# Output projection by one level of Strassen, in a hybrid attention layer on one core

## The chip, the core and the metric

The kernel runs on one core of one Trainium2 chip. Its engines have queues of their own, in order: TensorE (PE in the profile, PEld its weight loads), VectorE (DVE), ScalarE (ACT), GpSimd (POOL) and SyncE (SP), which here issues nearly all DMA transfers. Matmuls write to PSUM; GpSimd has only SBUF operands in this kernel. The metric is the device time of one execution in microseconds.

## The reference

One layer of a decoder trunk, in float32: 1024 tokens, model width 2048, batch 1. `x` is normalised, projected to 6656 columns, and goes through two groups of 16 heads (stick-breaking attention and sliding-window attention with sinks and a relative bias). What matters here is the end:

```python
o_sb = rmsnorm(o_sb, gn_sb[l]) * jax.nn.silu(z_sb)
o_sw = rmsnorm(o_sw, gn_sw[l]) * jax.nn.silu(z_sw)
y = jnp.einsum('bse,ed->bsd', jnp.concatenate([o_sb, o_sw], axis=-1), w_out[l])
h = h + rmsnorm(y, norm_post[l])
```

Each `rmsnorm` divides a token's row by its root mean square over the width (1024 for a group, 2048 for y) and multiplies it with a gain. So a group's norm gives one factor per token and group.

## The kernel before

The kernel is written with a tile framework: the program names tiles from pools (a tag with a number of buffers), and the framework places them, sets the semaphores, and orders each engine's queue at build time, by the order in the program and by when its own model has the operands ready. Matmuls issued through `mm` (line 105) keep the program's order; those of the output projection (line 681) have no such mark.

**Precision.** Every float32 matmul that matters is done as three matmuls in the type float32r. An operand is cast on ScalarE (`hi`), the residual is formed on VectorE (`lo` = raw - hi), and hi x hi, hi x lo and lo x hi are accumulated in PSUM.

**Before the output projection.** Lines 258 to 657 do the input projection block by block (`proj`, 52 blocks of 128 columns) with the attention units woven between. x stands in SBUF as 32 tiles `xh0` ... `xl15` of pool `xp`, whose space the output projection uses again. The last blocks of the input projection are gates `z_sb`. `evac_z` (329) multiplies a head pair's output by gain and SiLU gate, writes it to DRAM as `ogd[tile]` (16 tiles of 128 mixed columns, by 1024 tokens), and sums squares into `accs` (GpSimd). The group factor is not applied there: `group_rms` (350) turns `accs` into `ssw` and `ssb`, [128 tokens, 8 blocks], with 8 one-column matmuls for each group.

**The output projection** (lines 635 to 790) runs over two halves of the tokens (`th`), four blocks of 512 model columns (`dc`), the two groups (`gi`: mixed tiles 8 to 15 are the sliding-window group, 0 to 7 the stick-breaking one), 8 tiles `e` of a group and 4 token tiles `tb` of 128:
- `split_wo` (638) loads a block [128 mixed, 512 model] of `w_out`, casts it (645) and forms the residual (647). It is called two or three blocks ahead of the matmuls. Three raw buffers (`wraw`), four pairs of hi and lo.
- `load_og` (666) loads a tile of gated attention outputs for half the tokens and splits it the same way. All 16 tiles of a half stay in SBUF.
- `mm_out` (678) issues three matmuls with 128 tokens as the stationary operand and 512 model columns moving. Four PSUM banks collect the 8 tiles of a group; eight banks in all.
- `evac_sw` (704) copies the first group's sum out of PSUM times the token's factor `ssw` (ScalarE, 707); `evac_sb` (710) adds the second group's sum times `ssb` (VectorE, 719), squares the row with a running sum (ScalarE, 720), and multiplies by the post-norm gain `gp` (GpSimd, 721).
- `finish` (723) forms the row factor of y, loads x (`xr`, two staging buffers `u`), multiplies, adds (737) and stores (738). It runs for the first half's tokens after `th` = 0, for the others tile by tile at the end.
- For the last column block of the second half, `hold_w` (693) keeps all 16 weight blocks in SBUF, so that the last loop can go token tile by token tile; the very last sum goes in two parts of 256 columns.

Weight blocks are loaded and split again for the second half of the tokens: 128 loads and splits in all.

## Time and profile before

| | |
|---|---|
| median of 3 runs | 1888.94 us (1888.36 to 1891.02) |
| the profiled execution: its own time | 1889.21 us |
| its span in the trace | 1887.5 us |
| mean granted TensorE clock | 0.991 |
| DMA over the span | 236.94 MB, 126 GB/s |
| instructions | 26831 |

The span is that of the instructions; the execution's own time has a little around it. Busy times of engines add up what an engine worked on, side by side with the others; they say where work is, not what sets the time. What sets it is read from TensorE's idle times and what ended them, and from the chain of waits that ends last. Matmuls overlap: each is shown with some 0.39 us, but they follow each other more closely, so their cost is the distance between starts.

### The profile page before, as it was taken

How to read it: one execution, taken by the hardware profiler on the slowest of the kernel's cores; microseconds unless marked ns; L12 is line 12 of the kernel's file. 1: busy time of each engine (PE TensorE's matmuls, PEld its weight loads, DVE VectorE, ACT ScalarE, POOL GpSimd, SP SyncE). 2: the span in 40 equal slices, each digit the busy share in tenths (PEclk: the TensorE clock that was granted, in tenths of full speed). 3: DMA queues.
4: the chain of work that ended last, by engine and by line, in shares of the span. 5: the costliest groups of instructions: out<-in, count | busy, mean ns of one | idle time of the engine just before them, and what ended most of it. 6: DMA issues, size and time to landing. Idle time of an engine off the chain costs nothing.

```text
span 1887.5 us, 26831 instructions
## 1 busy us (share of the span) xinstructions
PE 1832.6 (97%) x9262; PEld 1533.1 (81%) x9262; DVE 1156.8 (61%) x1905; ACT 776.0 (41%) x1654; POOL 402.2 (21%) x440
## 2 busy tenths in 40 slices
PE   8799999999999999999999999999999999998997
PEld 6678888888888878888888888888888778886776
DVE  8548842688277685785667756577686743344433
ACT  6335531455244343443434444344343443332331
POOL 7411010101023141141221311113144311111111
PEclk9899999999999999999999999999999999999999
DMA  6545542455333243343333423334234743347435
GB/s 212 169 127 166 142 140 84 121 147 153 94 110 120 73 134 101 94 123 89 116 105 100 119 80 116 106 96 126 80 119 133 259 148 103 97 131 211 127 92 156
DMA packets 167255, 236.94 MB, mean 126 GB/s; under 512 B 21936, under 2 KB 81488, under 8 KB 166992
## 3 DMA queue, kind: packets, MB, share of 16 engines
q1 hardware_dynamic: 165056, 232.09, 42.6%
q10 hardware_dynamic: 2064, 3.15, 0.5%
q8 instruction: 73, 1.20, 0.3%
q14 instruction: 62, 0.51, 0.1%
HBM read 171.19 MB, written 63.96 MB: 125 GB/s over the span
## 4 chain that ended last, share of the span: by engine, by line
PE 77%; DMA 10%; DVE 6%; issue 2%; POOL 2%; ACT 2%; SPq 1%; DVEq 0%; ACTq 0%; POOLq 0%
PE p_ksb L110 9%; PE y L681 9%; PE p_qsb L110 9%; PE p_vsb L110 9%; PE p_qsw L110 8%; PE p_zsw L110 8%; PE p_zsb L110 6%; PE o_sb L110 4%; PE z_sb L110 4%; DMA woraw<-in_w_out 3%; DMA xr<-in_x 3%; PE wt_sb L114 3%; PE z_sw L110 2%; PE o_sw L110 2%; DVE m_sb L450 1%
## 5 line engine op out<-in xcount | busy, mean ns | idle before, releaser
L681 PE MATMUL y<-wohi,og 128*128 128x512 f32 x896 | 282.0, 394 | 7.5 <-ACT wohi L645 7.5
L681 PEld LDWEIGHTS y<-wohi,og 128*128 128x128 f32 x896 | 170.3, 190 | 46.4 <-ACT wohi L645 11.4
L450 DVE TENSOR_TENSOR_SCAN m_sb<-m_sb,zero 128x256 f32<-128x256 f32 x192 | 165.3, 902 | 62.3 <-ACT m_sb L439 61.2
L681 PE MATMUL y<-wolo,og 128*128 128x512 f32 x448 | 178.8, 399 | 8.9 <-DVE wolo L647 8.9
L439 ACT ACTIVATE m_sb<-z_sb 128x512 f32<-128x512 f32 x160 | 96.2, 601 | 148.6 <-PE z_sb L110 142.1
L647 DVE TENSOR_TENSOR wolo<-woraw,wohi 128x512 fp32r<-128x512 f32 x112 | 85.3, 770 | 112.6 <-ACT wohi L645 112.6
L445 POOL TENSOR_SCALAR_AFFINE_SELECT b_sb<-b_sb 128x512 f32<-128x512 f32 x64 | 49.9, 779 | 449.9 <-ACT b_sb L441 449.9
L450 DVE TENSOR_TENSOR_SCAN m_sb<-m_sb,mask 128x256 f32<-128x256 f32 x128 | 115.5, 939 | 43.8 <-ACT m_sb L439 43.3
L645 ACT CAST wohi<-woraw 128x512 fp32r<-128x512 f32 x112 | 68.5, 620 | 140.5 <-PE y L681 102.4
L454 DVE TENSOR_TENSOR b_sb<-b_sb,m_sb 128x512 f32<-128x512 f32 x160 | 111.0, 694 | 17.9 <-POOL b_sb L445 5.7
L721 POOL TENSOR_TENSOR y<-y,gp 128x512 f32<-128x512 f32 (+1 forms) x33 | 46.4, 1432 | 319.7 <-ACT y L720 319.7
L681 PEld LDWEIGHTS y<-wolo,og 128*128 128x128 f32 x448 | 85.2, 190 | 33.8 <-DVE wolo L647 16.6
L110 PE MATMUL p_zsw<-xh,whi_zsw 128*128 128x512 f32 x256 | 104.8, 409 | 0.0
L110 PE MATMUL p_ksb<-xh,whi_ksb 128*128 128x512 f32 x256 | 104.4, 408 | 0.0
L110 PE MATMUL p_qsb<-xh,whi_qsb 128*128 128x512 f32 x256 | 104.4, 408 | 0.0
L110 PE MATMUL p_zsb<-xh,whi_zsb 128*128 128x512 f32 x256 | 102.9, 402 | 0.0
L110 PE MATMUL p_vsb<-xh,whi_vsb 128*128 128x512 f32 x256 | 102.7, 401 | 0.0
L110 PE MATMUL p_zsw<-xh,wlo_zsw 128*128 128x512 f32 x256 | 101.1, 395 | 0.0
L110 PE MATMUL p_zsw<-xl,whi_zsw 128*128 128x512 f32 x256 | 101.0, 395 | 0.0
L110 PE MATMUL p_qsb<-xh,wlo_qsb 128*128 128x512 f32 x256 | 100.8, 394 | 0.0
L110 PE MATMUL p_ksb<-xh,wlo_ksb 128*128 128x512 f32 x256 | 100.7, 393 | 0.0
L110 PE MATMUL p_qsb<-xl,whi_qsb 128*128 128x512 f32 x256 | 100.6, 393 | 0.0
(237 smaller groups left out, 4786.7 us busy)
## 6 DMA issues: line engine op xcount, KB each, us to landing
woraw<-in_w_out SPq DMA_DIRECT2D x128, 256.0 KB, 3.2
kh<-kd SPq DMA_DIRECT2D x160, 64.0 KB, 2.5
kl<-kd SPq DMA_DIRECT2D x160, 64.0 KB, 2.5
q_sw<-qd SPq DMA_DIRECT2D x64, 128.0 KB, 3.2
od<-ot_sw SPq DMA_DIRECT2D x128, 64.0 KB, 2.2
or_zsw<-od SPq DMA_DIRECT2D x16, 512.0 KB, 4.1
wraw_qsb<-in_w_blk SPq DMA_DIRECT2D x32, 256.0 KB, 3.3
wraw_ksb<-in_w_blk SPq DMA_DIRECT2D x32, 256.0 KB, 3.1
```

The costliest lines, as they stand in the source:

```text
L110: tc.keep_in_program_order(nc.tensor.matmul(ps, a, b, start=start, stop=stop))
L114: tc.keep_in_program_order(nc.tensor.transpose(ps, a, ident))
L439: nc.scalar.activation(m[:, :, 1:257], z, AF.Sigmoid, scale=-SCALE)
L445: nc.gpsimd.affine_select(out=beta, in_=beta, compare_op=ALU.is_gt, fill=0.0, base=0, pattern=[[-P, 2], [1, 256]], channel_multiplier=-1)
L450: nc.vector.tensor_tensor_scan(m[:, tb, 1:257], m[:, tb, 1:257], mask[:, P - P * tb:P - P * tb + 256] if prev is None else zero.to_broadca ...
L454: nc.vector.tensor_mul(beta, beta, m[:, :, 0:256])
L645: nc.scalar.copy(wh, raw)
L647: nc.vector.tensor_sub(wl, raw, wh.bitcast(F32))
L681: nc.tensor.matmul(ps, ogt[:, a, cols], w, start=(first and i == 0), stop=(last and i == 2))
L721: nc.gpsimd.tensor_mul(yc, yc, gp[:, dc * HALF:(dc + 1) * HALF][:, part])
```

## The change

The output projection becomes one level of Strassen's scheme. The token halves (512 tokens), the halves of the mixed width (the two groups, 1024 each) and the halves of the model width (1024) make quarters of both operands; seven products of quarter sums replace the eight quarter products.
- The factors of the group norms can no longer be applied per group while evacuating, since sums run across groups. So `group_rms` now makes rows: a matmul of an all-ones [128, 128] tile (the first 128 columns of `mask`, all ones there) with `accs` gives each partition the factor of every token, [128, 1024] for each group; the attention outputs are multiplied with it when they are loaded.
- `PRODUCTS` lists, for each product, the quarters of x and their sign, those of the weights and theirs, and the quarters of y that it goes to, with sign and whether it is the last contribution.
- `split_wo` loads one or two parts of `w_out`; two are added or subtracted on GpSimd ahead of cast and residual. Two-part blocks have four pair buffers (two for the first eight blocks).
- `load_quarter` loads the four quarters of x once (products 1 and 2) and multiplies them with the factor rows, on VectorE and GpSimd in turn. `make_x` forms the sum (VectorE), cast and residual of an operand tile for the next product, in the second half of a product; 9 tiles.
- `evac` copies a first contribution to y out of PSUM (ScalarE) and adds or subtracts later ones (VectorE); a last contribution is followed by square and gain.
- `finish` runs for the second token half after product 6, for the first one tile by tile in the last half product. The last half product has 8 weight tiles of its own in place of `hold_w`.

The diff, cut to its core:

```diff
-    ssw = const.tile([P, 8], F32, name="ssw")
-    ssb = const.tile([P, 8], F32, name="ssb")
+    row_sw = const.tile([P, S], F32, name="row_sw")
+    ones = mask[:, :P]
...
-    def group_rms(grp, dst):
-        ps = pz(f"rms_{grp}")
-        for i in range(8):
-            mm(ps[:, i:i + 1], accs[grp][:, i * P:(i + 1) * P], one, start=True, stop=True)
-        nc.scalar.activation(dst, ps[:, 0:8], AF.Sqrt, bias=eps, scale=1.0 / 1024)
-        nc.vector.reciprocal(dst, dst)
+    def group_rms(grp, row):
+        for h in range(2):
+            cols = slice(h * HALF, (h + 1) * HALF)
+            ps = pz(f"rms_{grp}_{h}")
+            mm(ps, ones, accs[grp][:, cols], start=True, stop=True)
+            nc.scalar.activation(row[:, cols], ps, AF.Sqrt, bias=eps, scale=1.0 / 1024)
+            nc.vector.reciprocal(row[:, cols], row[:, cols])
...
-                defer(12.0, lambda: group_rms("sw", ssw))
+                defer(12.0, lambda: group_rms("sw", row_sw))
...
-    wo_list = [(th, dc, e) for th in range(2) for dc in range(4 - th) for e in list(range(8, 16)) + list(range(8))]
-    wo_ready = {}
...
+    Q_W = {"11": (8, 0), "12": (8, 1), "21": (0, 0), "22": (0, 1)}
+    Q_X = {"11": (8, 0), "12": (0, 0), "21": (8, 1), "22": (0, 1)}
+    PRODUCTS = [
+        (("11",), ("12", -1, "22"), (("12", 1, 0), ("22", 1, 0))),
+        (("21", -1, "11"), ("11", 1, "12"), (("22", 1, 0),)),
+        (("11", 1, "12"), ("22",), (("12", 1, 1), ("11", -1, 0))),
+        (("21", 1, "22"), ("11",), (("21", 1, 0), ("22", -1, 0))),
+        (("22",), ("21", -1, "11"), (("21", 1, 1), ("11", 1, 0))),
+        (("11", 1, "22"), ("11", 1, "22"), (("22", 1, 1), ("11", 1, 0))),
+        (("12", -1, "22"), ("21", 1, "22"), (("11", 1, 1),)),
+    ]
+    LAST = len(PRODUCTS) - 1
+    w_list = [(i, dc, e) for i in range(LAST + 1) for dc in range(2) for e in range(8)]
+    w_ready = []
+    out_pools = {}
+
+    def w_part(dst, quarter, dc, e):
+        e0, half = Q_W[quarter]
+        col = half * 2 * HALF + dc * HALF
+        nc.sync.dma_start(dst, w_out[(e0 + e) * P:(e0 + e + 1) * P, col:col + HALF])
 
     def split_wo(n):
-        for i in range(len(wo_ready), min(n, len(wo_list))):
-            th, dc, e = wo_list[i]
-            raw = load_wo(e, dc, f"{th}_{dc}_{e}")
-            alt = i % 2 if i >= 16 else 0
-            wp = (wr, stg)[alt]
-            wh = wp.tile([P, HALF], F32R, tag=("whi", "hi")[alt], name=f"wohi{th}_{dc}_{e}")
-            nc.scalar.copy(wh, raw)
-            wl = wp.tile([P, HALF], F32R, tag=("wlo", "sg")[alt], name=f"wolo{th}_{dc}_{e}")
-            nc.vector.tensor_sub(wl, raw, wh.bitcast(F32))
-            wo_ready[wo_list[i]] = wh, wl
+        for k in range(len(w_ready), min(n, len(w_list))):
+            i, dc, e = w_list[k]
+            terms = PRODUCTS[i][1]
+            nm = f"{i}_{dc}_{e}"
+            if len(terms) == 1 or not out_pools:
+                raw = wr.tile([P, HALF], F32, tag="wraw", name=f"woraw{nm}", bufs=3)
+                w_part(raw, terms[0], dc, e)
+                if len(terms) > 1:
+                    more = wr.tile([P, HALF], F32, tag="wraw", name=f"womore{nm}", bufs=3)
+                    w_part(more, terms[2], dc, e)
+            else:
+                if k >= 8 and k % 4 >= 2:
+                    pair = xp.tile([P, 2, HALF], F32, tag=out_pools["pairs"][k % 2], name=f"wopair{nm}")
+                else:
+                    pair = out_pools["at2"].tile([P, 2, HALF], F32, tag="wp", name=f"wopair{nm}", bufs=2)
+                raw, more = pair[:, 0, :], pair[:, 1, :]
+                w_part(raw, terms[0], dc, e)
+                w_part(more, terms[2], dc, e)
+            if len(terms) > 1:
+                (nc.gpsimd.tensor_add if terms[1] > 0 else nc.gpsimd.tensor_sub)(raw, raw, more)
+            if i == LAST and dc == 1:
+                t = out_pools["xp"].tile([P, 2, HALF], F32R, tag=out_pools["last"][e], name=f"wolast{e}")
+                hi, lo = t[:, 0, :], t[:, 1, :]
+            else:
+                alt = k % 2 if k >= 8 else 0
+                pool = (wr, stg)[alt]
+                hi = pool.tile([P, HALF], F32R, tag=("whi", "hi")[alt], name=f"wohi{nm}")
+                lo = pool.tile([P, HALF], F32R, tag=("wlo", "sg")[alt], name=f"wolo{nm}")
+            nc.scalar.copy(hi, raw)
+            nc.vector.tensor_sub(lo, raw, hi.bitcast(F32))
+            w_ready.append((hi, lo))
...
-    gp = at2.tile([P, D], F32, tag="gp", name="gp", bufs=1)
-    nc.sync.dma_start(gp, g_post.partition_broadcast(P))
...
+    R_TAGS = {"11": xtags[0:4], "21": xtags[4:8], "12": xtags[8:12], "22": xtags[12:16]}
+    Y_TAGS = {"12": xtags[16:20], "22": xtags[20:24], "11": xtags[24:28], "21": xtags[4:8]}
+    out_pools.update(at2=at2, xp=xp, pairs=xtags[30:32], last=xtags[0:4] + xtags[8:12])
+    gp = [xp.tile([P, 2 * HALF], F32, tag=xtags[28 + h], name=f"gp{h}") for h in range(2)]
...
+    def load_quarter(q, e):
+        e0, th = Q_X[q]
+        if e % 2 == 0:
+            held[q, e // 2] = xp.tile([P, 2, HALF], F32, tag=R_TAGS[q][e // 2], name=f"r{q}_{e}")
+        dst = held[q, e // 2][:, e % 2, :]
+        nc.sync.dma_start(dst, ogd[e0 + e][:, th * HALF:(th + 1) * HALF])
+        eng = nc.vector if e % 2 else nc.gpsimd
+        eng.tensor_mul(dst, dst, rows_of[e0][:, th * HALF:(th + 1) * HALF])
+
+    def quarter(q, e):
+        return held[q, e // 2][:, e % 2, :]
+
+    def make_x(i, e):
+        terms = PRODUCTS[i][0]
+        t = at2.tile([P, 2, HALF], F32R, tag="hl", name=f"x{i}_{e}", bufs=9)
+        hi, lo = t[:, 0, :], t[:, 1, :]
+        if i == 0:
+            src = stg.tile([P, HALF], F32, tag="u", name=f"xs{i}_{e}")
+            nc.sync.dma_start(src, ogd[8 + e][:, :HALF])
+            nc.gpsimd.tensor_mul(src, src, row_sw[:, :HALF])
+        elif len(terms) == 1:
+            src = quarter(terms[0], e)
+        else:
+            src = stg.tile([P, HALF], F32, tag="u", name=f"xs{i}_{e}")
+            (nc.vector.tensor_add if terms[1] > 0 else nc.vector.tensor_sub)(src, quarter(terms[0], e), quarter(terms[2], e))
+        nc.scalar.copy(hi, src)
+        nc.vector.tensor_sub(lo, src, hi.bitcast(F32))
+        return t
...
+    def evac(ps, i, tb, dc, part=slice(0, HALF)):
+        for q, sign, final in PRODUCTS[i][2]:
+            if (q, tb) not in ys:
+                ys[q, tb] = xp.tile([P, 2 * HALF], F32, tag=Y_TAGS[q][tb], name=f"y{q}_{tb}")
+            yc = ys[q, tb][:, dc * HALF:(dc + 1) * HALF][:, part]
+            if (q, tb, dc) not in seen:
+                seen[q, tb, dc] = True
+                nc.scalar.activation(yc, ps, AF.Copy, scale=float(sign))
+            else:
+                (nc.vector.tensor_add if sign > 0 else nc.vector.tensor_sub)(yc, yc, ps)
+            if final:
+                key = q[0], tb
+                if key not in st:
+                    st[key] = at2.tile([P, 4 + (key == ("1", 3))], F32, tag="st", name=f"st_{q}_{tb}", bufs=8)
+                    xq[key] = 0
+                nc.scalar.activation(sqt[:, part], yc, AF.Square, accum_out=st[key][:, xq[key]:xq[key] + 1])
+                xq[key] += 1
+                nc.gpsimd.tensor_mul(yc, yc, gp[int(q[1]) - 1][:, dc * HALF:(dc + 1) * HALF][:, part])
...
+    whole = slice(0, HALF)
+    xs = [make_x(0, e) for e in range(8)]
+    for i in range(LAST + 1):
+        nxt = []
+        for dc in range(2):
+            k0 = (2 * i + dc) * 8
+            if i == LAST and dc == 1:
+                split_wo(k0 + 8)
                 for tb in range(4):
+                    if tb < 3:
+                        ps = bank(f"y{i}_{dc}_{tb}")
+                        for e in range(8):
+                            mm_out(ps, xs[e], tb, w_ready[k0 + e], whole, e == 0, e == 7)
+                        evac(ps, i, tb, dc)
+                    else:
+                        last_x = stg.tile([P, 2, HALF], F32, tag="acc", name="last_x", bufs=1)
+                        nc.sync.dma_start(last_x, x[3 * P:4 * P, :D // 2].rearrange("p (a n) -> p a n", a=2))
+                        for h in range(2):
+                            part = slice(h * 256, (h + 1) * 256)
+                            ps = bank(f"y{i}_{dc}_{tb}_{h}")
+                            for e in range(8):
+                                mm_out(ps[:, :256], xs[e], tb, w_ready[k0 + e], part, e == 0, e == 7)
+                            evac(ps[:, :256], i, tb, dc, part)
+                    finish("1", tb)
+                continue
+            pss = [bank(f"y{i}_{dc}_{tb}") for tb in range(4)]
+            for e in range(8):
+                split_wo(k0 + e + 3)
+                for tb in range(4):
+                    mm_out(pss[tb], xs[e], tb, w_ready[k0 + e], whole, e == 0, e == 7)
+                if i == 0:
+                    for q in ("11", "21") if dc == 0 else ():
+                        load_quarter(q, e)
+                elif i == 1:
+                    for q in ("12",) if dc == 0 else ("22",):
+                        load_quarter(q, e)
+                if dc == 1 and i < LAST:
+                    nxt.append(make_x(i + 1, e))
+            if i == 0 and dc == 0:
+                group_rms("sb", row_sb)
+                for h in range(2):
+                    nc.sync.dma_start(gp[h], g_post[h * 2 * HALF:(h + 1) * 2 * HALF].partition_broadcast(P))
             for tb in range(4):
+                evac(pss[tb], i, tb, dc)
+        if i == LAST - 1:
+            for tb in range(4):
+                finish("2", tb)
+        xs = nxt
```

More of the change, by code (lines that the diff above doesn't have):

```diff
@@ new lines, in layer @@
+    row_sb = rstd
+    rows_of = {8: row_sw, 0: row_sb}
+    held = {}
+    def load_quarter(q, e):
[8 more added lines that the diff above has]
+        return held[q, e // 2][:, e % 2, :]
```

131 lines of the change are left out of this document (21 added, 110 removed).

## The prediction, made before the changed kernel ran

> **What bounds the kernel now.** I read the page's first part, then the one line of the output projection's matmuls, then the chain of waits, then windows of that stage.
>
> ```profile
> span 1887.5 us, 26831 instructions
> ...
> PE 1832.6 (97%) x9262; PEld 1533.1 (81%) x9262; DVE 1156.8 (61%) x1905; ACT 776.0 (41%) x1654; POOL 402.2 (21%) x440
> ```
>
> TensorE is busy nearly all of the span, so the time is the number of matmuls times their pitch, plus TensorE's waits. The matmuls of the output projection, with duration least/median/most in ns and first and last start:
>
> ```profile
> L681 PE MATMUL y<-wohi,og x896: 387/389/628, 1495.3 to 1830.8; 128*128 128x512 f32 x180
> L681 PE MATMUL y<-wolo,og x448: 387/389/796, 1495.5 to 1830.5; 128*128 128x512 f32 x150
> L681 PE MATMUL y<-wr,og x216: 277/389/389, 1831.0 to 1874.7; 128*128 128x512 f32 x84, 128*128 128x256 f32 x24
> ```
>
> Their number is 896 + 448 + 216 = 1560: 1512 of 512 columns and 48 of 256. They run from 1495.3 to 1875.0 us (the last row below ends there), 379.7 us. The pitch comes from the chain, where one piece is nothing but matmuls:
>
> ```profile
> 1525.95 149.78 PE y L681 x660
> ```
> ```profile
> 1857.74 17.25 PE L681 MATMUL y<-wr,og 128*128 128x512 f32 x98
> ```
>
> 149.78 / 660 = 0.2269 us per matmul of 512 columns. In the last row 50 of 512 columns take 11.3 us, and the 48 halves the other 5.9 us. So the matmuls alone are 1512 x 0.2269 + 5.9 = 349.0 us of the 379.7. The view of waits, TensorE's alone (total, times, longest):
>
> ```profile
> PE y L681 <- DVE wolo L647: 8.9, 17, 2.1
> PE y L681 <- ACT wohi L645: 7.5, 6, 2.1
> ```
>
> Of the other 31 us, 16.4 are waits for weight blocks being split.
>
> The same stage in windows (length, busy us and count of PE, PEld, DVE, ACT, POOL, then granted clock, DMA share, GB/s):
>
> ```profile
> 1500.00:1520.00 20.00, 17.88 (x66) 13.32 (x67) 16.10 (x22) 10.14 (x19) 6.42 (x5) 0.91 0.78 260
> 1520.00:1680.00 160.00, 160.00 (x715) 132.73 (x714) 55.63 (x80) 58.49 (x107) 18.81 (x14) 1.00 0.39 104
> 1680.00:1840.00 160.00, 147.50 (x610) 114.78 (x609) 67.58 (x95) 51.70 (x105) 22.34 (x15) 0.98 0.52 148
> 1840.00:1887.00 47.00, 34.99 (x177) 29.75 (x176) 16.19 (x29) 6.33 (x17) 5.27 (x5) 0.92 0.52 157
> ```
>
> While tokens of the first half run (1520 to 1680) TensorE never waits, with VectorE at 55.63 / 160 = 35%; afterwards the output stores and the held last weights cost it 12.5 us. Of granted clock, 20 x 0.09 + 160 x 0.02 = 5 us are lost before 1840. The timeline shows where (start, length, then in brackets the idle time before):
>
> ```profile
> 1500.22 0.49 PE L681 MATMUL y<-wohi,og 128*128 128x512 f32 x1 [2.05 <-ACT wohi L645]
> ...
> 1501.54 1.05 PE L681 MATMUL y<-wohi,og 128*128 128x512 f32 x2
> ...
> 1506.20 0.62 PE L681 MATMUL y<-wohi,og 128*128 128x512 f32 x2
> ```
>
> After 2.05 us of idling two matmuls take 1.05 us together, five microseconds later 0.62: the clock is halved for a while.
>
> The stage is bound by TensorE with everything else hidden; the question is what stays hidden.
>
> **The change: what TensorE saves.** Seven products of 192 matmuls (2 column blocks, 8 tiles of mixed width, 4 token tiles, 3 terms) are 1344, of which 24 become 48 halves. 1320 x 0.2269 + 5.9 = 305.4 us. The group factors as rows need two full-width matmuls against ones, where sixteen one-column passes stood:
>
> ```profile
> 1524.27 1.68 PE rms_sb L110 x16
> ```
> ```profile
> L256 DVE RECIPROCAL rstd<-rstd 128x512 f32<-128x512 f32 x2 | 6.6, 3323 | 0.8 <-ACT rstd L255 0.8
> ...
> L110 PE MATMUL ssq<-acc_x,ones 128*128 128x512 f32 x4 | 3.5, 1022 | 9.7 <-POOL acc_x L224 9.7
> ...
> L291 DVE TENSOR_TENSOR u_zsb<-p_zsb,rstd 128x512 f32<-128x512 f32 x16 | 10.8, 675 | 1.9 <-PE p_zsb L110 1.9
> ```
>
> The second row is the same sort of matmul at the kernel's start: 3.5 us for two. So TensorE needs 308.9 us instead of 349.0 + 1.7 = 350.7, a gain of **41.8 us** if nothing else becomes late.
>
> **What the other engines get.** Durations now, mean ns behind the bar:
>
> ```profile
> L647 DVE TENSOR_TENSOR wolo<-woraw,wohi 128x512 fp32r<-128x512 f32 x105 | 79.7, 768 | 112.1 <-ACT wohi L645 112.1
> L737 DVE SCALAR_TENSOR_TENSOR y<-y,rs,xr 128x512 f32<-128x512 f32 x16 | 13.5, 856 | 27.4 <-DMA xr<-in_x 27.1
> L699 DVE TENSOR_TENSOR wr<-woraw,wr 128x512 fp32r<-128x512 f32 x16 | 13.2, 827 | 45.4 <-ACT wr L698 45.4
> ...
> L721 POOL TENSOR_TENSOR y<-y,gp 128x512 f32<-128x512 f32 x28 | 41.2, 1498 | 282.0 <-ACT y L720 282.0
> ...
> L645 ACT CAST wohi<-woraw 128x512 fp32r<-128x512 f32 x104 | 63.6, 620 | 136.9 <-PE y L681 98.8 <-DMA woraw<-in_w_out 29.4 <-DVE y L737 6.7
> L707 ACT ACTIVATE y<-y,ssw 128x512 f32<-128x512 f32 x29 | 19.1, 688 | 4.2 <-PE y L681 4.0
> ```
>
> VectorE: 112 weight residuals (128 before), 56 residuals of x operands (32 before), 40 sums of x quarters, 16 of 32 quarters times a factor row, 32 final multiply-adds: 256 operations with two SBUF inputs. Added to that are 64 additions from PSUM into y, in the place of 32; L291 in the row above, which reads PSUM too, takes 0.675. Four row reciprocals at 3.32 us replace two tiny ones. GpSimd: 80 sums of weight quarters, 8 + 16 products with factor rows, 32 with the post-norm gain: 136, where 33 stood. ScalarE's casts and evacuations stay at some 0.62 and 0.69 us; even the fullest product has 16 + 8 casts, at most 8 evacuations and 8 squares, 26 us of 43.6, so it is no bound. SP issues 192 weight loads (two per summed block) instead of 128, 40 quarters instead of 32 and as many x and output transfers, 300 of them:
>
> ```profile
> 1477.81 0.33 SPq L632 DMA_DIRECT2D woraw<-in_w_out  x1
> ```
>
> At 0.33 us each that is some 100 us of the stage, hidden, unless one of them waits for its buffer with weight loads behind it.
>
>
> **The price of GpSimd beside VectorE.** Timeline, a GpSimd operation by itself and a VectorE subtraction by itself:
>
> ```profile
> 88.45 1.29 POOL L300 TENSOR_TENSOR u_ksw<-u_ksw,hi_ksw 128x512 f32<-128x512 f32 x1 [12.66 <-ACT hi_ksw L299]
> ```
> ```profile
> 1564.89 0.69 DVE L647 TENSOR_TENSOR wolo<-woraw,wohi 128x512 fp32r<-128x512 f32 x1 [2.03 <-ACT wohi L645]
> ```
>
> Alone they take 1.29 and 0.69 us. Where the two engines meet, and the same line alone:
>
> ```profile
> 1477.32 1.62 POOL L347 TENSOR_TENSOR acc_sb<-acc_sb,sg_zsb 128x512 f32<-128x512 f32 x1
> 1477.71 1.77 DVE L339 SCALAR_TENSOR_TENSOR u_zsb<-u_zsb,gsb,sg_zsb 128x512 f32<-128x512 f32 x1
> ```
> ```profile
> L339 DVE SCALAR_TENSOR_TENSOR u_zsb<-u_zsb,gsb,sg_zsb 128x512 f32<-128x512 f32 x1 | 0.7, 740 | 0.0
> ```
>
> VectorE's operation starts 0.39 us into GpSimd's and lasts 1.77 us where alone it lasts 0.74 (last row): a meeting costs VectorE 1.03 us. How often?
>
> ```profile
> 1698.68 0.76 DVE y L737
> ```
>
> L737 undisturbed is this 0.76. Between 1520 and 1840, L647, L737 and L699 exceed their undisturbed 0.69, 0.76 and 0.69 us by 8.2 + 1.5 + 2.2 = 11.9 us in all, beside 28 GpSimd operations: 0.42 us each, with VectorE 39% busy (123.2 of 320 us).
>
> Call c VectorE's loss per GpSimd operation. It lies between 0.42 (nothing gets worse with load) and 1.03 (every one hits). In the changed kernel VectorE is nearly full, so I take **c = 0.70**, about the middle.
>
> The Trainium skill, "SBUF — State Buffer", section "Who interferes with whom", states that a VectorE instruction with two SBUF inputs and a GpSimd instruction that reads SBUF exclude each other, and that the second one fully blocks. The trace agrees (1.77 against 0.74 us). Held for whole instructions, the two engines would need 136 x 1.29 + 256 x 0.69 = 352 us by that rule, an estimate above TensorE's 308.9; by the 1.03 us of the rows, 136 x 1.03 + 177 = 317.
>
> **Half by half.** A half product is 96 matmuls, 21.8 us. VectorE's queue in order: the residuals of the weight blocks for it, the x operand of the next product (all of it in the second half), the evacuation of the half before. With D its operations at 0.69 us and G those of GpSimd, D x 0.69 + G x 0.70 gives, over 21.8:
> - product 1, first half: 20 D (8 residuals, 8 factor rows, 4 of the first x; the other 4 lie ahead of 1495), 20 G: 27.8, over by 6.0. Second half: 24 D, two reciprocals 6.6, 8 G: 28.8, over by 7.0.
> - product 2: 12 D, 12 G: 16.7, hidden. Then 32 D (8 residuals, 16 for the next x, 4 factor rows, 4 evacuations), 12 G: 30.5, over by 8.7.
> - product 3: 8.3, then 28 D, 4 G: 22.1, over by 0.3. Product 4: 11.1 and 13.8, hidden.
> - product 5: 13.9; then 32 D (8 residuals, 16 for the next x, 8 evacuations), 12 G (8 sums, 4 gains): 30.5, over by 8.7.
> - product 6: 19.4, then the same 30.5, over by 8.7.
> - product 7, first half: 16 D, 8 of the 16 final multiply-adds at 0.76, 12 G: 25.5, over by 3.7.
>
> The sum is 43.1 us. It counts as TensorE's wait, since weights are only split three blocks ahead (8.2 us) and behind a late x operand in the same queue; what the light halves could take up of that lead I leave to the range, and with it the first x operands, which now pass two staging buffers that the last gate evacuation uses too (0 to 12 us late, 0 taken beyond the 6.0).
>
> Product 7, second half: its first token tile reads all 8 weight blocks within 24 matmuls, 5.4 us; they are made one per 2.72 us (12 x 0.2269), 21.8 us, with a lead of 8.2: **8 us** of waiting. Bounds 0 (they are made early, into tiles of their own) and 16 (no lead). The clock lost after waits I keep at 4 us (before: 5; bounds 0 and 15, some 20 new waits against few). The Trainium skill, "TensorE: Matmul & The Clock Gate", Part 1, has the clock drop only after an idle window of about 3.4 us, by which this term would be 0; the trace speaks against it, with a drop after 2.05 us. The sliding-window group's factor row costs TensorE the same 3.5 - 1.7 = 1.8 us during attention and puts 6.6 us of reciprocals into VectorE's queue there, with the residuals of transposed weights queued behind them, for which matmuls wait; between 0 and 6.6, I take 1.2, as VectorE is busy 61% of the span and can catch up: 3.0 together. The tail behind the last matmul, 1887.5 - 1875.0, has the same steps as before (evacuation, square, row factor, multiply-add, store): no change.
>
> Sum: 308.9 + 43.1 + 8 + 4 = 364.0 against 379.7, so -15.7, +3.0 = -12.7. The profiled execution's own time is 1889.2 (the median 1888.94 lies 0.3 below): **1876.5 us**.
>
> **Rivals.**
> 1. *The cover holds* (c = 0.42). Over by 0.4, 4.8, 5.3, 0, 5.3, 5.3, 0.3 = 21.4: 342.3, so 1889.2 - 37.4 + 3.0 = **1855**; with the spill into light halves some 10 less. For it: 1520 to 1680 without a wait. Against: 35% VectorE there, about 76% here ((320 x 0.69 + 13.2) / 308.9).
> 2. *Slower: the two engines block each other on every operation* (c = 1.03), in the second halves of products 1, 2, 5 and 6, where x operand, weight sums and gains meet. Over by 12.6, 9.6, 12.7, 1.6, 12.7, 1.6, 12.7 and 7.7 = 71.2: 392.1, so 1889.2 + 12.4 + 3.0 = **1905**. It decides from c = 0.85 on, where the excess reaches 56 us and the gain is gone. For it: VectorE's and GpSimd's work both lie before a weight block's residual, in queues in order, and a gain multiply that waits for a square holds up the next weight sum. Against: evacuations read PSUM and need not meet GpSimd. The page named above has the same thing as its rule.
> ```profile
> woraw<-in_w_out SPq DMA_DIRECT2D x128, 256.0 KB, 3.2
> ```
> ```profile
> 60.00:70.00 10.00, 4.58 (x21) 3.46 (x19) 1.54 (x3) 2.82 (x5) 5.30 (x4) 0.85 0.93 323
> ```
>
> 3. *Transfers bound product 7.* 32 weight loads and 32 loads and stores of the first finished tokens are 64 x 256 KB = 16.8 MB; at the 260 GB/s of the window 1500 to 1520, 64.5 us instead of 25.5 + 21.8 + 8 = 55.3: +9, so **1885**. Against it: a load of 256 KB lands in 3.2 us now (first row), and in the window of the second row the queues carried 323 GB/s.
>
> That fewer matmuls aren't issued is no case: the loops fix their number.
>
> **How the numbers follow.** The forecast has 0.40 (0.34 clearly faster, 0.06 next to no change), rival 1 has 0.22, rival 2 0.27, rival 3 0.11 (0.06 and 0.05). About 0.2%, 3.8 us, is what a measurement here can tell from no change: faster 0.34 + 0.22 + 0.06 = 0.62, same 0.06 + 0.05 = 0.11, slower 0.27. The range runs from within rival 1 to rival 2: 1850 to 1905. The likeliest case alone: 1862 to 1887.
>
> **What would show it.** Right: 1344 + 24 = 1368 matmuls at 0.227 us; waits of TensorE for VectorE's residuals, thick in the second halves of products 1, 2, 5, 6 and thin in 3 and 4; residuals with a mean of 1.0 us or more where GpSimd adds; some 8 us at the start of the last half. Wrong: waits that end with a DMA; residuals near 0.75 us (rival 1); VectorE over 95% busy in products 5 and 6 (rival 2); a pitch other than 0.227.

## The result, and the profile after

The changed kernel takes 1920.39 us (median; 1920.01 to 1921.63), 1.0163 times the time before (95% interval 1.0145 to 1.0181). It is slower by 1.6%, where 1876.5 was forecast, and lies above the range (1850 to 1905).

The page's first part, of the changed kernel:

```profile
span 1918.5 us, 26656 instructions
...
PE 1798.6 (94%) x9046; PEld 1500.3 (78%) x9046; DVE 1283.6 (67%) x2002; ACT 777.2 (41%) x1664; POOL 562.4 (29%) x544
```

TensorE is busy for 34 us less and the span is 31.0 us longer. The line of the output projection's matmuls (duration least/median/most in ns, first and last start) shows where to look:

```profile
L787 PE MATMUL y<-wohi,x x832: 387/389/796, 1515.8 to 1841.1; 128*128 128x512 f32 x167
...
L787 PE MATMUL y<-wolo,x x416: 389/389/793, 1516.4 to 1840.8; 128*128 128x512 f32 x139
...
L787 PE MATMUL y<-wolast,x x120: 277/389/628, 1841.7 to 1878.4; 128*128 128x512 f32 x72, 128*128 128x256 f32 x48
```

832 + 416 + 120 = 1368 matmuls, as forecast. They begin at 1515.8 (1495.3 before) and end at 1878.7, the last start and its 0.28 us. From first to last that is 362.9 us, against 379.7 before and 364.0 forecast. The matmuls fell in number as planned; the time went at both ends. Before the first matmul 20.5 us came on; behind the last one the span now runs another 39.8 us, where it ran 12.5. So 20.5 - 16.8 + 27.3 = **31.0 us**, the whole difference of the spans. The input projection ends at 1493.3 (1495.1 before): attention paid nothing for its row factor.

The same stage in windows, about one for a half product (length, busy us and count of PE, PEld, DVE, ACT, POOL, then granted clock, DMA share, GB/s):

```profile
1495.00:1516.00 21.00, 0.21 (x1) 0.22 (x2) 14.66 (x15) 2.38 (x4) 16.34 (x11) 0.55 0.76 266
1516.00:1551.00 35.00, 29.48 (x99) 20.52 (x100) 16.81 (x19) 11.53 (x20) 20.02 (x14) 0.88 0.72 224
1551.00:1586.00 35.00, 27.05 (x99) 20.28 (x99) 32.69 (x26) 13.54 (x23) 26.53 (x16) 0.90 0.68 208
...
1742.00:1763.00 21.00, 21.00 (x95) 17.38 (x94) 21.00 (x22) 9.09 (x19) 15.59 (x10) 1.00 0.51 147
1763.00:1790.00 27.00, 23.65 (x98) 19.06 (x97) 23.97 (x25) 9.06 (x19) 18.93 (x13) 0.94 0.59 180
...
1812.00:1841.00 29.00, 25.11 (x98) 19.81 (x97) 21.81 (x32) 7.52 (x19) 15.67 (x11) 0.88 0.73 225
1841.00:1879.00 38.00, 28.85 (x123) 21.53 (x121) 19.84 (x28) 9.43 (x22) 16.16 (x13) 0.91 0.76 219
1879.00:1918.00 39.00, 0.00 (x0) 0.00 (x0) 13.84 (x24) 2.02 (x9) 4.14 (x4) 0.55 0.69 204
```

TensorE is empty in the first and the last of these, and waits in product 1 (second and third row), product 6 (1763 to 1790) and product 7 (1812 to 1879). In these same rows the granted clock is below 1.00: 0.88, 0.90, 0.94, 0.88 and 0.91. From 1742 to 1763, the second half of product 5, VectorE is busy every microsecond, and TensorE still doesn't wait. The chain of waits has the dense piece between:

```profile
1597.30 141.54 PE y L787 x623
```

141.54 / 623 = 0.2272 us, the old pitch. TensorE's waits (total, times, longest):

```profile
PE y L787 <- ACT x L738: 23.0, 3, 22.1
PE y L787 <- DVE wolo L680: 19.0, 9, 4.4
PE y L787 <- ACT wolast L679: 7.9, 6, 2.8
```

The first row is the **start**: one wait of 22.1 us for the first x operand. The timeline, with the issues of SP, and of VectorE, GpSimd and ScalarE what stands in that operand's way (start, length, instruction):

```profile
1490.15 6.91 SPq L718 DMA_DIRECT2D r<-ogd  x11
...
1504.77 0.32 SPq L346 DMA_DIRECT2D ogd<-u_zsb  x1
...
1506.79 0.32 SPq L731 DMA_DIRECT2D xs<-ogd  x1
```
```profile
1498.94 1.74 DVE L720 TENSOR_TENSOR r<-r,row_sw 128x512 f32<-128x512 f32 x1
...
1504.06 0.69 DVE L338 TENSOR_TENSOR u_zsb<-u_zsb,or_zsb 128x512 f32<-128x512 f32 x1
...
1513.82 1.26 POOL L732 TENSOR_TENSOR xs<-xs,row_sw 128x512 f32<-128x512 f32 x1
...
1515.12 0.62 ACT L738 CAST x<-xs 128x512 fp32r<-128x512 f32 x1 [9.10 <-POOL xs L732]
```

The load of the operand (L731) is issued at 1506.79, behind a store of the gate's result (L346), which waits for VectorE (L338, done at 1504.75). VectorE is late with it, since quarters for product 2 that SP loaded first (L718) are multiplied by the factor row in between, and meet GpSimd: 1.74 us for one. The load also needs one of the two `u` buffers, and the gate's result stands in one until its store has landed: the load is issued 2.0 us after that store, and in that stretch such stores took 2.1 us to land. The load, three operations of the last gate that stand ahead on GpSimd (1509.64 to 1513.86), GpSimd's multiply and the cast then take the other 9 us.

The **tail** is the mirror of that. SP's waits, and the end of the chain of waits:

```profile
SPq L759 <- DVE y L758: 48.2, 28, 4.7
```
```profile
1889.83 4.85 DMA xr<-in_x
...
1894.70 0.76 DVE y L758
...
1895.48 0.33 SPq L759
...
1895.91 3.75 DMA xr<-in_x
```

The chain is a round: load of x, multiply-add, store, and only then the next load, as the store stands ahead of it in SP's queue and the load needs one of two `u` buffers. Two tiles at a time go round in turn, 30 tiles between 1814 and 1913. Before the change half of these tiles had the second half's whole run of matmuls to hide under. Now the first 16 come after product 6, and the last loads of these are issued only here:

```profile
1869.24 1.66 SPq L756 DMA_DIRECT2D xr<-in_x  x2
```

Only two of the other 14 follow before TensorE is done at 1878.7; 12 rounds are left for the tail. Transfers aren't the limit: 204 to 225 GB/s in the last three windows, 266 in the first.

### The profile page after: what moved, and what is told of

Its sections match the earlier page's. It is cut to its first block, busy times and chain, and to the rows that moved or that the text cites. A ratio compares the mean times of both kernels' runs of the same rounds, so it can differ in the third digit from the quotient of the medians.

```text
span 1918.5 us, 26656 instructions
## 1 busy us (share of the span) xinstructions
PE 1798.6 (94%) x9046; PEld 1500.3 (78%) x9046; DVE 1283.6 (67%) x2002; ACT 777.2 (41%) x1664; POOL 562.4 (29%) x544
## 4 chain that ended last, share of the span: by engine, by line
PE 74%; DVE 11%; DMA 8%; POOL 4%; issue 2%; ACT 2%; SPq 1%; POOLq 0%; DVEq 0%; ACTq 0%
PE p_ksb L110 9%; PE p_vsb L110 9%; PE p_qsb L110 8%; PE p_qsw L110 8%; PE y L787 7%; PE p_zsw L110 7%; PE p_zsb L110 7%; PE o_sb L110 4%; PE z_sb L110 3%; PE wt_sb L114 3%; DMA xr<-in_x 3%; DMA wopair<-in_w_out 2%; DVE wolo L680 2%; DVE m_sb L449 2%; PE z_sw L110 1%
## 5 line engine op out<-in xcount | busy, mean ns | idle before, releaser
L787 PE MATMUL y<-wohi,x 128*128 128x512 f32 x832 | 267.0, 401 | 25.1 <-ACT x L738 23.0
L787 PEld LDWEIGHTS y<-wohi,x 128*128 128x128 f32 x832 | 161.5, 194 | 62.9 <-ACT x L738 24.5
L787 PE MATMUL y<-wolo,x 128*128 128x512 f32 x416 | 168.2, 404 | 19.1 <-DVE wolo L680 19.0
L670 POOL TENSOR_TENSOR wopair<-wopair 128x512 f32<-128x512 f32 x78 | 120.6, 1550 | 126.2 <-DMA wopair<-in_w_out 115.8
L453 DVE TENSOR_TENSOR b_sb<-b_sb,m_sb 128x512 f32<-128x512 f32 x160 | 112.8, 705 | 18.2 <-POOL b_sb L444 6.1
L787 PEld LDWEIGHTS y<-wolo,x 128*128 128x128 f32 x416 | 80.8, 194 | 41.1 <-DVE wolo L680 24.3
L110 PE MATMUL p_vsb<-xh,wlo_vsb 128*128 128x512 f32 x256 | 100.5, 393 | 0.5 <-DVE wlo_vsb L123 0.5
L110 PE MATMUL p_zsb<-xh,wlo_zsb 128*128 128x512 f32 x256 | 100.5, 393 | 0.0
```

Source lines behind the costliest of these rows:

```text
L110: tc.keep_in_program_order(nc.tensor.matmul(ps, a, b, start=start, stop=stop))
L453: nc.vector.tensor_mul(beta, beta, m[:, :, 0:256])
L670: (nc.gpsimd.tensor_add if terms[1] > 0 else nc.gpsimd.tensor_sub)(raw, raw, more)
L787: nc.tensor.matmul(ps, xt[:, a, tc_], w[b][:, cols], start=first and n == 0, stop=last and n == 2)
```

## Experiments

The table gives all the kernels, each from one trace, in us: from the start of the input projection's last matmul to that of the output projection's first; what product 1, products 2 to 6 and the first half of product 7 took beyond 96 x 0.2267 = 21.76 us for each half; the length of the last half (24 matmuls are 48 halves there: 22.2 without a wait); from the start of the last matmul to the end. A loss is all that is beyond the matmuls' pitch: waits, matmuls at a lower granted clock and, in product 1, the factor row's own matmuls. Ratios are to the kernel before, with 95% intervals.

| kernel | start | product 1 | 2 to 6 | 7, first half | last half | tail | ratio |
|---|---|---|---|---|---|---|---|
| changed | 22.4 | 26.7 | 8.9 | 7.5 | 36.7 | 40.1 | 1.0163 (1.0145-1.0181) |
| xr8 | 21.6 | 24.6 | 13.1 | 23.7 | 29.4 | 19.8 | 1.0138 (1.0123-1.0153) |
| first_own | 2.7 | 32.4 | 11.6 | 8.0 | 37.0 | 38.9 | 1.0145 (1.0128-1.0161) |
| both | 2.8 | 32.5 | 14.9 | 23.9 | 29.1 | 20.0 | 1.0099 (1.0082-1.0116) |
| nosum | 18.2 | 19.9 | 0.0 | 0.6 | 33.8 | 46.8 | 1.0046 (1.0033-1.0059) |
| noxr | 22.2 | 26.9 | 10.5 | 16.5 | 29.1 | 11.2 | 1.0043 (1.0028-1.0058) |
| start | 2.7 | 25.7 | 11.7 | 25.1 | 29.6 | 20.5 | 1.0067 (1.0043-1.0092) |
| nostore2 | 21.6 | 26.3 | 10.7 | 19.1 | 32.4 | 9.4 | 1.0065 (1.0044-1.0086) |
| reorder | 2.8 | 30.9 | 24.9 | 0.8 | 32.3 | 8.7 | 0.9964 (0.9952-0.9977) |
| spread | 1.2 | 31.6 | 7.9 | 4.5 | 26.9 | 9.2 | 0.9874 (0.9853-0.9895) |
| spread_start | 3.1 | 21.6 | 14.6 | 5.1 | 28.3 | 8.6 | 0.9867 (0.9849-0.9884) |
| sums_dve | 0.2 | 19.9 | 11.7 | 4.0 | 29.5 | 9.5 | 0.9864 (0.9841-0.9886) |
| sums_dve_odd | 2.2 | 22.0 | 16.2 | 0.7 | 32.5 | 8.7 | 0.9883 (0.9863-0.9904) |

### The two ends, each by itself and together

**xr8**: eight buffers for x in `finish` in place of two, in the dead tiles of a quarter.

```diff
-                xr = stg.tile([P, HALF], F32, tag="u", name=f"xr_{t}_{dc}")
+                if dc % 2 == 0:
+                    xrt[0] = xp.tile([P, 2, HALF], F32, tag=R_TAGS["22"][(2 * t + dc // 2) % 4], name=f"xr_{t}_{dc}")
+                xr = xrt[0][:, dc % 2, :]
```

> x for the final sum is staged in eight buffers (the four tiles that held x quarter 22, dead by then) instead of the two u buffers. Theory (the stores' chain x load, multiply-add, store through two buffers sets the end): the time behind the last matmul falls from 39.8 us to 12 to 16 us and the whole to about 1895 us. Rival (the end is bound by the transfers themselves, some 14 MB in all in the last 100 us): the tail stays above 30 us, the whole above 1912 us. Rival (VectorE and GpSimd together bound the last product): the tail falls, but the last matmul comes later, the whole stays above 1908 us.

**first_own**: the first operands come from the quarter that product 1 reads anyway, with no staging and no second load.

```diff
         if i == 0:
-            src = stg.tile([P, HALF], F32, tag="u", name=f"xs{i}_{e}")
-            nc.sync.dma_start(src, ogd[8 + e][:, :HALF])
-            nc.gpsimd.tensor_mul(src, src, row_sw[:, :HALF])
-        elif len(terms) == 1:
+            load_quarter("11", e)
+        if len(terms) == 1:
...
-                    for q in ("11", "21") if dc == 0 else ():
+                    for q in ("21",) if dc == 0 else ():
```

> The operand tiles of product 1 are made from the loaded and scaled quarter 11, whose tiles are free early, instead of from a second load of the same data through the two u buffers; eight loads and eight GpSimd products less. Theory (the first operand waits for buffers that the last gate evacuation holds, and behind quarter loads that were put ahead of it): the wait before the first output matmul falls from 22.1 us to under 6 us, the whole to about 1900 us. Rival (the stage starts late because VectorE and GpSimd are full there): the wait stays above 15 us, or the 27 us lost in product 1 grow by what the wait loses; the whole above 1912 us.

**both**: the two edits together.

> Both edits. Theory: they add up, 1920 - 25 - 20 = about 1875 us, faster than before (1889). Rival (one cause hides another): less than three quarters of the sum, above 1886 us.

Measured: 1911.67, 1914.25 and 1904.21 us; the theories had 1895, 1900 and 1875, and all three missed. Each edit removes its own place, but most of the gain is lost elsewhere. xr8's tail falls from 40.1 to 19.8, but the first half of product 7 loses 23.7 instead of 7.5. SP's issues in xr8 show why:

```profile
1816.38 12.02 SPq L648 DMA_DIRECT2D wopair<-in_w_out  x5
1829.24 8.04 SPq L761 DMA_DIRECT2D out<-y  x8
1837.33 2.38 SPq L758 DMA_DIRECT2D xr<-in_x  x5
...
1849.42 0.85 SPq L648 DMA_DIRECT2D wopair<-in_w_out  x2
```

With eight buffers 13 of the 16 stores of the second token half and 8 loads of x go in one piece, and no weight is loaded between 1828.4 and 1849.4. The two slow buffers of the changed kernel had let weight loads in between. first_own ends the wait at the start (2.7 us), but product 1 loses 32.4 instead of 26.7 and products 2 to 6 2.7 more; the likely cause, which no run separates, is that the loads and multiplies that the wait had covered now stand in front of product 1. The input projection also ended 6.6 us later in that kernel's trace, at 1499.9; among all the traces it ends between 1493.3 and 1499.9, which none of these runs explains.

### What the ends consist of

**nosum**: GpSimd's 80 sums left out.

```diff
-            if len(terms) > 1:
-                (nc.gpsimd.tensor_add if terms[1] > 0 else nc.gpsimd.tensor_sub)(raw, raw, more)
```

> The changed kernel with the 80 GpSimd sums of weight parts left out; both parts are still loaded, the first alone is used. Theory of the prediction (VectorE loses time to GpSimd): the 26.7 us lost in product 1 fall below 15, the 13 us lost in the halves from 11 to 13 go, the whole falls by 15 us or more. Theory now (transfers and the order of their queue set the start and the end): the wait of 22 us and the tail of 40 us stay within 3 us, the whole falls by less than 10 us.

**noxr**: the loads of x in `finish` left out.

```diff
-                xr = stg.tile([P, HALF], F32, tag="u", name=f"xr_{t}_{dc}")
-                nc.sync.dma_start(xr, x[t * P:(t + 1) * P, dcols])
...
-            nc.vector.scalar_tensor_tensor(yc, yc, rs, xr, op0=ALU.mult, op1=ALU.add)
+            nc.vector.scalar_tensor_tensor(yc, yc, rs, yc, op0=ALU.mult, op1=ALU.add)
```

> The changed kernel with the loads of x for the final sum left out (the final operation adds y itself). Theory now (32 loads of x, with the stores behind them in the queue, set the end): the tail falls from 40 us to 12 to 15 us and product 7 loses less than the 7.5 and 9 us of now, the whole falls by 30 us or more. Rival (VectorE and GpSimd bound product 7): product 7 loses as much as before; the whole falls by 25 us at most.

**nostore2**: xr8, with the 16 stores of the second token half left out.

```diff
-            nc.sync.dma_start(out[t * P:(t + 1) * P, dcols], yc)
+            if q == "1":
+                nc.sync.dma_start(out[t * P:(t + 1) * P, dcols], yc)
```

> As xr8, with the 16 stores of the second token half left out (512 rows of the output are not written). xr8 lost 23.7 us in the first half of product 7. Theory (the stores stand in the transfer queue and wait for VectorE, weight loads behind them): the loss falls to 10 us or less. Rival (the burst of 16 multiply-adds on VectorE holds up the weight residuals by itself): it stays above 16 us.

Measured: 1893.64, 1893.96 and 1899.17 us. Neither expectation of nosum held whole: the later halves went as the first one said, but product 1 kept more than 15 us, and the whole fell by 1.2%, more than the second one allowed. noxr fell by as much, some 23 us, and went its rival's way, and so did nostore2 (19.1, above 16).

Without sums products 2 to 6 lose nothing and the first half of product 7 0.6, against 8.9 and 7.5: nearly all that TensorE lost there came with the sums: by their meetings with VectorE, or by their step in the chain of a weight block. The final sums of the second token half are in nosum too, at the pace of two buffers, and cost next to nothing there. Product 1 still loses 19.9, and the tail grows to 46.8: TensorE is done earlier, and the rounds of x are not. Without loads of x the tail is 11.2, like before the change (12.8 in this measure): the round is what lengthened the tail. But the first half of product 7 loses 16.5 in noxr, with no x in the queue at all. Its SP issues, and VectorE beside them:

```profile
1807.28 19.54 SPq L648 DMA_DIRECT2D wopair<-in_w_out  x12
1827.67 13.99 SPq L754 DMA_DIRECT2D out<-y  x16
1841.78 5.09 SPq L648 DMA_DIRECT2D wopair<-in_w_out  x8
```
```profile
1826.06 11.93 DVE L753 SCALAR_TENSOR_TENSOR y<-y,rs 128x512 f32<-128x512 f32 x12
```

Sixteen stores in a row, each waiting for a multiply-add of VectorE's burst, hold the weight loads for 14 us. Is it the stores? nostore2 keeps 19.1 of xr8's 23.7: no, they are 4.6 us of it. With them gone the same burst holds up the x loads, which need its buffers, and the weight loads behind them. SP in nostore2:

```profile
1828.93 8.16 SPq L758 DMA_DIRECT2D xr<-in_x  x10
1838.32 0.81 SPq L648 DMA_DIRECT2D wopair<-in_w_out  x2
```

So it is the 16 final sums put in one place, ahead of weight blocks in VectorE's and SP's queues, whichever of their transfers is left.

### Moving the final sums

**reorder**: first_own with the products in another order, so that the second token half is complete after product 5; x is staged in eight buffers, the dead tiles of quarter 11, the last weights lie in the tiles of 12 and 22, and quarter 22 is loaded ahead of 12.

```diff
         (("21", -1, "11"), ("11", 1, "12"), (("22", 1, 0),)),
-        (("11", 1, "12"), ("22",), (("12", 1, 1), ("11", -1, 0))),
-        (("21", 1, "22"), ("11",), (("21", 1, 0), ("22", -1, 0))),
+        (("11", 1, "22"), ("11", 1, "22"), (("22", 1, 0), ("11", 1, 0))),
+        (("21", 1, "22"), ("11",), (("21", 1, 0), ("22", -1, 1))),
         (("22",), ("21", -1, "11"), (("21", 1, 1), ("11", 1, 0))),
-        (("11", 1, "22"), ("11", 1, "22"), (("22", 1, 1), ("11", 1, 0))),
+        (("11", 1, "12"), ("22",), (("12", 1, 1), ("11", -1, 0))),
...
-        if i == LAST - 1:
+        if i == LAST - 2:
```

> First operands as in first_own, and the products in another order, so that the second token half is finished after product 5 instead of 6, with a one-part product next; eight staging buffers for x from the tiles of quarter 11. The same sums. Theory (25 MB of loads and stores crowd into product 7 and the tail): from the start of the last product to the end 75 us or less instead of 95 to 106, the whole about 1885 us. Rival (product 7 is bound by its weight blocks): the last product and the tail stay above 88 us, the whole above 1898 us.

**spread**: reorder, with the four token tiles of that half finished after blocks 4 and 8 of the two halves of product 6.

```diff
-        if i == LAST - 2:
-            for tb in range(4):
-                finish("2", tb)
...
+                if i == LAST - 1 and e % 4 == 3:
+                    finish("2", 2 * dc + e // 4)
```

> As reorder, with the final sums of the four token tiles given out over product 6, after blocks 4 and 8 of each half, instead of all ahead of it. Theory (a burst of sums and stores ahead of the weight loads costs the 20.5 us that reorder loses in the first half of product 6): the loss falls under 6 us, the whole to about 1865 us. Rival (transfers: 48 of 256 KB in product 6 take the time): it loses 12 us or more over product 6 still.

Measured: 1879.15 and 1863.95 us, against some 1885 and 1865 expected: both theories held. reorder frees the tail (8.7) and product 7's first half (0.8); the burst, in one piece still, now costs 20.5 us in the first half of product 6, of the 24.9 in the table. Its SP queue, with no weight load for 16.6 us (1763.1 to 1779.7):

```profile
1754.43 8.68 SPq L648 DMA_DIRECT2D woraw<-in_w_out  x2
1764.42 4.97 SPq L759 DMA_DIRECT2D out<-y  x8
1769.44 2.40 SPq L756 DMA_DIRECT2D xr<-in_x  x5
...
1779.73 0.85 SPq L648 DMA_DIRECT2D woraw<-in_w_out  x2
```

Cut into four, the same work leaves that half 2.2 us of loss, and product 7's first half 4.5. The kernel is 1.3% faster than before the change and 2.8% faster than the changed one (0.9874 / 1.0163). Moving the burst, with eight buffers for x, freed the tail but moved the burst's price in among the matmuls; cutting it up ended most of it.

### Product 1

**start**: both, with the loads of the quarters for later products queued behind the store of the last gate.

```diff
+        if q == "11":
+            nc.sync.dma_start(dst, ogd[e0 + e][:, th * HALF:(th + 1) * HALF])
+        else:
+            with tc.issue_after(gate_store[0].ins):
+                nc.sync.dma_start(dst, ogd[e0 + e][:, th * HALF:(th + 1) * HALF])
```

> As both, and the loads of x quarters 21, 12 and 22 are queued behind the last gate's store, so that their products with the factor rows no longer stand ahead of that gate on VectorE. Theory (the store waits for VectorE at the head of the transfer queue, weight loads behind it): the first half of product 1 loses under 10 us instead of 19.9, the whole falls by 8 to 12 us against both. Rival (two pair buffers for the first eight blocks, or GpSimd, bound product 1): it loses 17 us or more still.

**spread_start**: spread with that order, and all four pair buffers and both pairs of hi and lo in use from block 4 on (8 before).

```diff
-                if k >= 8 and k % 4 >= 2:
+                if k >= 4 and k % 4 < 2:
...
-                alt = k % 2 if k >= 8 else 0
+                alt = k % 2 if k >= 4 else 0
```

> As spread, with quarters 21, 12 and 22 loaded behind the last gate's store as in start, and four pair buffers and both pairs of hi and lo from weight block 4 on instead of block 8. Theory (queue order and two pair buffers cost product 1 its 31 us): product 1 loses under 15 us, 12 to 16 us less than spread. Rival (product 1 has 20 GpSimd products and sums and 52 loads at once; VectorE and GpSimd bound it): it loses 22 us or more.

Measured: 1897.67 and 1861.71 us. start takes 7 us off product 1 (25.7 against 32.5 in both). Its first half still loses 15.0, between theory (10) and rival (17), and the whole falls by 0.3%, some 6 us, less than the 8 to 12 expected. In spread_start product 1 loses 21.6 instead of 31.6, also between theory (15) and rival (22), but products 2 to 6 give back 7, and against spread the intervals overlap: no gain that can be told.

### Whose sums

**sums_dve**: spread_start with all 80 sums on VectorE. **sums_dve_odd**: every second one (`if k % 2` in place of `if True`).

```diff
-                (nc.gpsimd.tensor_add if terms[1] > 0 else nc.gpsimd.tensor_sub)(raw, raw, more)
+                eng = nc.vector if True else nc.gpsimd
+                (eng.tensor_add if terms[1] > 0 else eng.tensor_sub)(raw, raw, more)
```

> As spread_start, with all 80 sums of weight parts on VectorE instead of GpSimd. In the changed kernel each GpSimd operation cost VectorE some 0.65 us; a sum on VectorE costs 0.69. Theory (the meeting is the price): VectorE's work stays about the same and GpSimd's queue is gone from the chain, the whole within 6 us of spread_start (1856 to 1868). Rival (VectorE's own work is the price, meetings are hidden): each two-part half product gets 8 more operations, 5.5 us, ten of them: 15 us slower or more, above 1877 us.

> As spread_start, with every second sum on VectorE. Theory: half of that, within 4 us of spread_start, or a few us faster as neither queue is as long. Rival: 7 us slower or more, above 1869 us.

Measured: 1860.98 and 1865.61 us, the same as spread_start within the intervals, as the theories had it. The window 1590 to 1850, spread_start first, then sums_dve:

```profile
1590.00:1850.00 260.00, 248.76 (x1084) 203.41 (x1083) 203.38 (x262) 104.08 (x211) 131.68 (x88) 0.98 0.64 197
```
```profile
1590.00:1850.00 260.00, 242.22 (x1057) 197.69 (x1055) 202.12 (x311) 102.77 (x211) 44.70 (x33) 0.97 0.61 187
```

VectorE has 311 operations instead of 262 and is busy as long, 202.1 us. GpSimd's 87 us of sums bought nothing. The residuals of summed blocks, again spread_start first, then sums_dve (mean ns behind the bar):

```profile
L681 DVE TENSOR_TENSOR wolo<-wopair,wohi 128x512 fp32r<-128x512 f32 x70 | 77.6, 1118 | 27.3 <-ACT wohi L680 26.3
```
```profile
L682 DVE TENSOR_TENSOR wolo<-wopair,wohi 128x512 fp32r<-128x512 f32 x70 | 54.4, 785 | 4.0 <-ACT wohi L681 3.9
```

## Why the prediction was wrong

Forecast were 12.7 us less and 31.0 more came, 43.7 us off. Two terms that the sum put at nothing make more than all of that: the start (20.5 us) and the tail (27.3). From first to last matmul the sum came out at 362.9 us of 364.0, but by luck: the waits were forecast some 11 us too high (51.1, some 40 came) and the lost clock 12 us too low.

**TensorE's need: right.** There are 1368 matmuls at the old pitch. The factor row's matmuls took 1.7 us instead of 3.5.

**c = 0.70: near.** In the changed kernel, from 1720 to 1812, VectorE's operations with two SBUF inputs exceed their undisturbed times by 27.3 us in all, beside 42 GpSimd operations: 0.65 us each. From 1516 to 1841 it is 66 us beside 108, 0.61 each. In the residuals' line it is the mean of 1057 ns that was named as its sign:

```profile
L680 DVE TENSOR_TENSOR wolo<-wopair,wohi 128x512 fp32r<-128x512 f32 x70 | 73.3, 1057 | 30.2 <-ACT wohi L679 29.6
```

Rival 2 (c from 0.85) is out by it, and so is rival 1. That rival 2's 1905 us lies nearest to the result is luck: its mechanism isn't what made the time.

**"The clock lost after waits I keep at 4 us": mis-sized, 12 us.** By the prediction's own working, the length of a window times what its granted clock lacks to 1.00, the changed kernel loses 35 x 0.12 + 35 x 0.10 + 27 x 0.06 + 29 x 0.12 + 38 x 0.09 = 16.2 us between 1516 and 1879, above the upper bound of 15. This is at most: some of the slow time falls on waits and costs nothing there. 63 matmuls of these stretches follow each other at twice the pitch, which is 12.6 us.

**"Half by half": too high, and wrong in its places.** Forecast were 43.1 us of waiting in the first 13 halves. The same 43.1 came as loss, but up to 12.8 of it is the lost clock (the first four terms above) and 1.7 the factor row's matmuls, so that some 29 are waits. Product 1 has 26.7 of the loss, 7.7 of it clock, and so some 17 of waiting (13.0 forecast); products 2 to 7 have 16.4, up to 5.1 of it clock, and so some 11 (30.1 forecast). The step that failed is "It counts as TensorE's wait": an overfull half need not make TensorE wait, most likely because it eats the lead of the weight blocks first. The second half of product 5, with VectorE busy 21.00 of 21 us, cost nothing in itself; in the next half, forecast as hidden, 5.3 were lost. The second half of product 2, over by 8.7 in the forecast, lost nothing. In product 1, where there is no lead yet, the sum fell short.

**The last half: a little more than forecast.** 36.7 - 22.2 = 14.5 came, 3.4 of it clock (the last term above), so some 11 of waiting against 8; 7.9 of it is the row of `wolast` among the waits.

**"The first x operands ... 0 to 12 us late, 0 taken beyond the 6.0": a term put at nothing, 20.5 us.** The bounds were too narrow also. The two staging buffers were weighed, and the trace shows them in it (the load goes out when the gate's store has landed). What was not weighed is that loads of a later product's quarters could come ahead in SP's queue, and their multiplies ahead of the gate on VectorE. first_own shows the term: without that staging and its second load the wait is 2.7 us. How much the buffers cost and how much the quarters, no run separates.

**"The tail behind the last matmul ... has the same steps as before: no change": a term put at nothing, 27.3 us.** The steps are the same; what is queued ahead of them isn't. The 16 x loads of the second token half through the same two buffers came right before the 14 of the first. xr8 and noxr show it: 19.8 and 11.2 us instead of 40.1.

**Rival 3** had the right place and the wrong resource. Product 7 is where 16 final sums meet the weights, but at 219 to 225 GB/s, not as a bound of transfers; it's the order in one queue and VectorE's burst (noxr, nostore2), and in four pieces the burst costs little (spread).

**Attention's row factor, 3.0 us forecast:** the input projection ended 1.8 us earlier than before, so nothing of it shows; between traces that end varies by more.

Still open is what product 1 loses in the best versions, 20 to 22 us, the largest part left. Of the changed kernel's 26.7, up to 7.7 are lost clock and 1.7 the factor row's matmuls, as said above; 7 went with the sums (nosum, 19.9); start took 7 from both; sums_dve has meetings left in that stage, 14.7 us of VectorE's time over 17 GpSimd operations. How much is that, how much the loads of quarters (252 GB/s over 1495 to 1590 in sums_dve) and how much the factor row's reciprocals, no run separates.

## What to carry to other kernels

When a change shortens the engine that bounds a stage, price the stage's two ends first: which transfers now stand ahead of the first operand in its queue, and how much finishing work is left when the bound engine is done. Price the clock too: here it was below 1.00 in most stretches with waits and at 1.00 in those without, and that cost 12 us more than forecast. Count what an in-order queue carries between two weight loads, buffers and all: a store that waits for compute holds every load behind it, and more buffers made that piece longer here, so cut such work and put it between the blocks. Work handed to GpSimd beside a full VectorE need not be off VectorE: here the sums cost the same on either.

## What the runs showed of the hardware

The meeting of VectorE and GpSimd is nearly all or nothing. Of 211 VectorE operations with two SBUF inputs from 1516 to 1841 in the changed kernel, 139 are shown with under 0.8 us and 47 with 1.7 or more. The chain of waits of the changed kernel, VectorE at work without a pause:

```profile
1760.47 0.60 DVE x L739
1761.08 1.70 DVE wolo L680
1762.78 0.60 DVE xs L737
```

An operation adds 0.60 us when it is let through and 1.70 when it isn't: a meeting costs 1.10 us, and a sum of the same size done by VectorE itself adds some 0.60. With c = 0.61 to 0.65 on average, that fits that sums on VectorE are no dearer. The Trainium skill, "SBUF — State Buffer", section "Who interferes with whom", states that a VectorE instruction with two SBUF inputs contends with a GpSimd instruction that reads SBUF; the traces agree and add the price, almost that of two further operations.
